# A macaron decoder layer on one core: FFN1's gain row and the gate weights loaded in an earlier group, and one late addition put behind the first block's rows

## The chip, the cores and the metric

The kernel runs on one core of a Trainium2 chip. The metric is the device time of one execution in microseconds (us). The core has a matrix engine, TensorE (PE; its weight loads are listed apart as PEld), a vector engine, VectorE (DVE), an engine for activation functions and scaled copies, ScalarE (ACT), a general engine, GpSimd (POOL), and a synchronising engine, SyncE (SP), which here only issues DMA transfers. POOL issues DMA transfers too, from its own queue. Every engine executes its instructions in program order and waits on semaphores for the others. 16 DMA engines move the data between HBM and the on-chip memory SBUF. Products of TensorE land in PSUM, eight banks of 128 x 512 float32.

## What is computed

One layer of a hybrid decoder: a half-step SwiGLU FFN, a mixer (a gated linear recurrence beside sliding-window attention), and a second half-step FFN, each between an RMSNorm on its input and one on its output. 512 tokens, width 1024, FFN width 2816, float32.

```python
def rms_norm(x, g):
    xf = x.astype(jnp.float32)
    y = xf * lax.rsqrt(jnp.mean(xf * xf, axis=-1, keepdims=True) + RMS_EPS)
    return (y * g.astype(jnp.float32)).astype(x.dtype)

def swiglu(x, w_gu, w_down):
    gate, up = jnp.split(x @ w_gu, 2, axis=-1)
    return (jax.nn.silu(gate) * up) @ w_down
...
    for l in range(DEPTH):
        x = x + 0.5 * rms_norm(swiglu(rms_norm(x, ffn1_pre_g[l]), ffn1_w_gu[l], ffn1_w_down[l]), ffn1_post_g[l])
        y = hybrid_mixer(rms_norm(x, mix_pre_g[l]), w_in[l], conv_w[l], conv_b[l], w_rg[l], b_rg[l],
                         w_ig[l], b_ig[l], lru_lambda[l], sinks[l], g_lru_out[l], g_attn_out[l], w_o[l])
        x = x + rms_norm(y, mix_post_g[l])
        x = x + 0.5 * rms_norm(swiglu(rms_norm(x, ffn2_pre_g[l]), ffn2_w_gu[l], ffn2_w_down[l]), ffn2_post_g[l])
```

In the mixer, `w_rg` and `w_ig` are block-diagonal gate weights, eight blocks of 64 x 64 each.

## The kernel before, in words

**Numbers.** Every float32 operand of a product is split into a high and a low part, and a product is three passes of TensorE: high times high, high times low, low times high. ScalarE makes the high parts (`act.copy`, the tiles `whi...`, `hha...`), VectorE the low parts (`wlo...`, `hla...`). The class `Weights` loads raw weights by SP into a ring of buffers and casts them a few units ahead of their use. A call of `take` hands the next unit to TensorE, and `W.later(n, fn)` registers a function that is issued after the n-th take from then on.

**FFN1.** Hidden columns are worked in groups of four chunks of 128 (`octo`, with seven products of half size in place of eight). The last group is `octo(16)`. Its result lies in `sqa` and is dealt into four blocks, `a11`, `a12`, `a21`, `a22` (tiles `ha`), by 16 small DMAs on SP and 16 on POOL (`place`, L992). The group before is multiplied with its down weights by `SevenDown.run`. Its partial sums are added to what earlier groups summed: some by a DMA that accumulates (L1105, POOL's queue, tiles `yp_a<-stage`), some by VectorE (L1097).

**The late addition.** In the last group `run` has `keep` set, and the banks of the last products stay in PSUM. For form `s1` the loop `for half in range(1 + i)` at L1095 adds bank 0 once and bank 1 twice, to the parts (1, 1) and (3, 1), counted by block of 128 tokens and half of the columns. The addition to part (3, 1) (`yp_a31`) also has to wait for an accumulating DMA to that part. It is the third of the three additions, and the part is not read before block 3.

**The end of FFN1, `boundary`.** The four blocks of 128 tokens are finished one by one. `produce(tb, dh)` issues the last down products of block `tb` and column half `dh`. `Rows.piece` adds the partial sum, squares it on ScalarE with a running sum (`sqyr`, L675), and multiplies by the gain row on VectorE (`zr`, L700). `Rows.steps` makes the residual sum (`x_rows`, L708) and the next norm (`sqxr`, `xn_r`). `Rows.turn` transposes the block on TensorE (`tp_r`, L729). TensorE runs ahead: the products of blocks 0 and 1 need only `a11` and `a12`; those of blocks 2 and 3 need `a21` and `a22`, and `whole.split` of these (L1397 on ScalarE, L1398 on VectorE) is issued in `produce(1, 0)`, behind all rows of block 0. `split_gates` (L1304 on ScalarE, L1305 on POOL) is issued in `produce(0, 1)`, ahead of block 0's second half. After the blocks, the first products of the mixer follow (`an`, L780, weights `whi_xl`, `wlo_xl`).

**Loads.** The constructor of `Rows` loads the gain row, spread over 128 partitions, into two tiles (L670, `grow_r`), and `load_gates` clears two tiles on POOL (L1295) and loads the gate weights into them by four DMAs on SP (L1298). Both are called after `octos` has issued the whole last group and its down products, so in SP's queue they stand behind the 16 DMAs of `ha`. All these tiles come from one ring of 41 buffers of 2 KB a partition (`t2k`): a load waits until the last reader of its buffer's former tile is done.

**FFN2** ends in the same way, in a loop of its own at the end of the program (L1923 on); its three additions to `yp_b` are at L1097 too, its gain row at L1920, its split of `a21` and `a22` after block 0's rows.

Of the kernel before, what the change touches and what calls it, by code (L numbers as in the profile page):

```python
# [15 lines left out]
P = 128  # L16
T = 512
NB = T // P
D = 1024
# [102 lines left out]
def tile_layer(ctx: ExitStack, tc: tile.TileContext, out: bass.AP, **ins: bass.AP):  # L122
# [465 lines left out]
    class Turned:  # L588
# [64 lines left out]
        def blocks(self):  # L653

            l, r = HALF
            for k in range(4):
# [2 lines left out]
                    pool.dma_start(b11[:, sl], x[:, l])  # L659
                self.t["b11", k] = b11[:, l], b11[:, r]  # L660

    class Rows:


        def __init__(self, name, x, gain, scale, eps, nxt, store=None):
            self.name, self.x, self.scale, self.eps, self.nxt, self.store = name, x, scale, eps, nxt, store
            self.z, self.ss, self.xn, self.tp = {}, {}, {}, {}
            self.grow = [t2k(f"grow_{name}{dh}") for dh in range(2)]
            for dh in range(2):
                sync.dma_start(self.grow[dh], ins[gain][0:1, dh * T:(dh + 1) * T].to_broadcast([P, T]))  # L670

        def sum_square(self, tb, dh, src, name):
            if dh == 0:
# [359 lines left out]
    class SevenDown:  # L1033
# [41 lines left out]
        def run(self, one, part, rest, keep=False):  # L1075
# [3 lines left out]
            for name, form, blocks in (("a", "a11", []), ("d", "s3", [(1, 1)]), ("b", "a12", [(0, 0)]), ("a", "s2", [(1, 0)]),  # L1079
# [10 lines left out]
                for i in range(2):  # L1090
                    if keep and form in ("a12", "s4", "a22"):
                        (half, dh), = blocks
                        kept[2 * half + i, dh] = banks[i]
                    elif keep and form == "s1":
                        for half in range(1 + i):  # L1095
                            o = part(half, 1, i)
                            dve.tensor_add(o, o, banks[i])  # L1097
                        if not i:
                            kept[2, 1] = banks[i]
                    else:  # L1100
                        st = wt("stage")
                        act.copy(st, banks[i])  # L1102
                        for half, dh in blocks:
                            o = part(half, dh, i)
                            pool.dma_start(o, st, accum_op=ALU.add)  # L1105
# [250 lines left out]
        for n, step in zip(takes, steps):  # L1356
            W.later(n, hid.place, step)

    def octos(hid, f0, f1, in_hbm, early=None):

        order = ("a11", "+s3", "s3", "a12", "+s1", "+s2", "s2", "+s4", "s4")
        parts = {}
        for f in range(f0, f1, 4):
            last = f == f1 - 4
            if last:
                for q in range(f1, FC, 2):
                    hid.quad(q, False, AHEAD)
                W.later(11, lambda: parts.update(read_parts(hid.name, in_hbm)))
            if f > f0:
                down = SevenDown(hid, f - 4)  # L1370
                down.ahead(zip((6, 6, 7, 8, 9, 9, 10, 11, 12) if f == f0 + 4 else (1, 2, 3, 4, 5, 6, 7, 8, 9), order))
# [92 lines left out]
    def produce(tb, dh):  # L1464
# [450 lines left out]
    for i in range(2):  # L1915
        load_rows(i, x_hbm, pool)
    preload(AF.Sqrt)
    grow = [t2k(f"grow{dh}") for dh in range(2)]
    for dh in range(2):
        sync.dma_start(grow[dh], ins["ffn2_post_g"][0:1, dh * T:(dh + 1) * T].to_broadcast([P, T]))  # L1920

    last = Last(f0, f1)
    for tb in range(NB):  # L1923
# [23 lines left out]
        if not tb:  # L1947
            for name in ("a21", "a22"):
                whole.split(name)
        if end:  # L1950
            dve.tensor_add(tot, tot, ss[:, 2:3])
        else:
            dve.tensor_add(tot, ss[:, 0:1], ss[:, 1:2])
# [36 lines left out]
```

## Time and profile before

| | us |
|---|---|
| median of three runs | 844.05 (843.65 to 845.2) |
| the profiled execution | 843.01 |
| its span, first to last instruction | 841.3 |
| TensorE busy | 821.8 (98%) |
| VectorE busy | 708.2 (84%) |
| ScalarE busy | 540.4 (64%) |
| GpSimd busy | 235.7 (28%) |
| mean granted clock of TensorE | 0.993 |

The times of rows in the profile are us from the span's start. A row of a timeline has start, duration, engine, source line, operation, `output<-inputs` by the program's names (without buffer numbers), the shape, and in brackets the engine's idle time before it with what ended that. The granted clock is the share of TensorE's full clock that the chip allowed it. A DMA share over 1 comes from transfers that overlap on one engine.

### The profile page before, as it was taken

The numbers are of one execution on the slowest core, as the hardware profiler recorded it, in microseconds if no ns is written. First come the engines' busy times: TensorE is split into PE (matmuls) and PEld (weight loads), VectorE is DVE, ScalarE is ACT, GpSimd is POOL, SyncE is SP. The second block draws the span as 40 slices with busy tenths as digits, with TensorE's granted clock in tenths as the row PEclk, the third lists the DMA queues.
The fourth block names the chain that finished last, engine by engine and source line by source line (L and its number), as shares of the span: only waits on it lengthen the run. The fifth ranks groups of instructions, "written<-read, shape, count | busy, mean of one in ns | idle before, by whom it ended". The sixth has DMA issues, their size and how long they took to land.

```text
span 841.3 us, 12066 instructions
## 1 busy us (share of the span) xinstructions
PE 821.8 (98%) x4156; PEld 693.4 (82%) x4156; DVE 708.2 (84%) x963; ACT 540.4 (64%) x905; POOL 235.7 (28%) x331
## 2 busy tenths in 40 slices
PE   9999999999999996999999999999999999999995
PEld 8888888888898885898788879888888888888884
DVE  4988889989979965767888767898998998899966
ACT  6756656665767563657857777674667677577542
POOL 2022004180460271005303103130418036055172
PEclk9999999999999998999999999999999999999998
DMA  8355316498694578032041344362549959589383
GB/s 251 102 194 206 132 69 203 115 206 253 145 240 118 198 183 231 10 92 95 6 101 51 125 175 176 136 209 106 157 148 209 263 136 202 188 195 245 140 210 113
DMA packets 90977, 133.22 MB, mean 158 GB/s; under 512 B 10600, under 2 KB 40612, under 8 KB 90916
## 3 DMA queue, kind: packets, MB, share of 16 engines
q1 hardware_dynamic: 69460, 91.41, 33.7%
q0 software_dynamic: 21312, 40.92, 22.6%
q8 instruction: 32, 0.52, 0.3%
q14 instruction: 29, 0.24, 0.1%
q10 hardware_dynamic: 144, 0.13, 0.0%
HBM read 93.10 MB, written 26.74 MB: 142 GB/s over the span
## 4 chain that ended last, share of the span: by engine, by line
PE 45%; ACT 6%; DVE 5%; DMA 1%; issue 1%; SPq 1%; POOL 0%; DVEq 0%; ACTq 0%
PE ab L935 12%; PE db L935 6%; PE bb L935 3%; PE an L780 1%; DMA x_rows<-x_hbm 1%; PE wo L1859 1%; PE mn L780 1%; PE yab L1336 1%; PE yab L1334 1%; PE yab L1335 1%; PE an L481 1%; PE gt L461 1%; PE sc L1571 1%; PE gt L463 1%; PE gt L462 1%
## 5 line engine op out<-in xcount | busy, mean ns | idle before, releaser
L1105 POOL DMA_DIRECT2D yp_b<-stage x46 | 44.6, 1308 | 93.4 <-ACT stage L1102 93.1
L992 POOL DMA_DIRECT2D hb<-sqb x80 | 48.4, 697 | 61.2 <-PE db L935 35.0
L992 POOL DMA_DIRECT2D ha<-sqa x64 | 39.0, 699 | 52.7 <-DVE sqa L950 44.4
L1105 POOL DMA_DIRECT2D yp_a<-stage x32 | 31.1, 1284 | 63.4 <-ACT stage L1102 60.6
L935 PE MATMUL aa<-whi_a_p,b_a 128*128 128x512 f32 x64 | 19.7, 389 | 0.0
L935 PE MATMUL ab<-whi_b_p,b_f 128*128 128x512 f32 x64 | 19.7, 389 | 0.0
L1522 POOL TENSOR_TENSOR xcl<-xc,xch 128x512 fp32r<-128x512 f32 x4 | 5.1, 1295 | 46.4 <-ACT xch L1521 46.4
L1610 POOL TENSOR_SCALAR_AFFINE_SELECT pc<-pa 128x384 f32<-128x384 f32 x8 | 5.6, 717 | 44.3 <-ACT pa L1609 43.6
L935 PE MATMUL db<-whi_b_q,t13h_f 128*128 128x512 f32 x40 | 15.6, 389 | 0.0
L935 PE MATMUL db<-whi_b_q,t13l_f 128*128 128x512 f32 x40 | 15.6, 389 | 0.0
L935 PE MATMUL db<-wlo_b_q,t13h_f 128*128 128x512 f32 x40 | 15.6, 389 | 0.0
L935 PE MATMUL ab<-whi_b_r,t24h_f 128*128 128x512 f32 x40 | 15.6, 389 | 0.0
L935 PE MATMUL ab<-whi_b_r,t24l_f 128*128 128x512 f32 x40 | 15.6, 389 | 0.0
L935 PE MATMUL ab<-wlo_b_r,t24h_f 128*128 128x512 f32 x40 | 15.6, 389 | 0.0
L935 PE MATMUL bb<-whi_b_s,xh_f 128*128 128x512 f32 x40 | 15.6, 389 | 0.0
L935 PE MATMUL bb<-whi_b_s,xl_f 128*128 128x512 f32 x40 | 15.6, 389 | 0.0
L935 PE MATMUL bb<-wlo_b_s,xh_f 128*128 128x512 f32 x40 | 15.6, 389 | 0.0
L935 PE MATMUL ab<-whi_b_t,t13h_f 128*128 128x512 f32 x40 | 15.6, 389 | 0.0
L935 PE MATMUL ab<-whi_b_t,t13l_f 128*128 128x512 f32 x40 | 15.6, 389 | 0.0
L935 PE MATMUL ab<-wlo_b_t,t13h_f 128*128 128x512 f32 x40 | 15.6, 389 | 0.0
L935 PE MATMUL db<-whi_b_u,t24h_f 128*128 128x512 f32 x40 | 15.6, 389 | 0.0
L935 PE MATMUL db<-whi_b_u,t24l_f 128*128 128x512 f32 x40 | 15.6, 389 | 0.0
(1536 smaller groups left out, 3266.0 us busy)
## 6 DMA issues: line engine op xcount, KB each, us to landing
yp_b<-stage POOLq DMA_DIRECT2D x54, 256.0 KB, 6.2
yp_a<-stage POOLq DMA_DIRECT2D x40, 256.0 KB, 6.6
raw_ad<-in_ffn_w_down SPq DMA_DIRECT2D x4, 1024.0 KB
hb<-sqb SPq DMA_DIRECT2D x80, 32.0 KB, 4.2
hb<-sqb POOLq DMA_DIRECT2D x80, 32.0 KB, 4.1
xn<-in_x SPq DMA_DIRECT2D x8, 256.0 KB, 3.0
ha<-sqa SPq DMA_DIRECT2D x64, 32.0 KB, 4.2
ha<-sqa POOLq DMA_DIRECT2D x64, 32.0 KB, 3.9
```

Of the source, the lines that this page charges most:

```text
L461: pe.matmul(ps, hi[:, k, :], xh, start=start, stop=False)
L462: pe.matmul(ps, hi[:, k, :], xl, start=False, stop=False)
L463: pe.matmul(ps, lo[:, k, :], xh, start=False, stop=stop)
L481: pe.matmul(sl(ps), w[:, k, :], xh, start=False, stop=False, skip_group_check=True)
L780: pe.matmul(l(b), w[part][:, k, :], l(xs[k][xpart]), start=k + part + xpart == 0, stop=stop and k == KD - 1)
L935: pe.matmul(o, x, w[:, k, :], start=first and i + k + j == 0, stop=i == 1 and k == 1 and j == 2, skip_group_check=True)
L992: (sync if i else pool).dma_start(o, squares[rows, 8 * pair + q:8 * pair + q + 5:4].rearrange("f c b t -> f c (b t)"))
L1105: pool.dma_start(o, st, accum_op=ALU.add)
L1334: pe.matmul(banks[i], hh[:, js], hi[:, k, :], start=first and k == 0, stop=False, skip_group_check=True)
L1335: pe.matmul(banks[i], hh[:, js], lo[:, k, :], start=False, stop=False, skip_group_check=True)
L1336: pe.matmul(banks[i], hl_[:, js], hi[:, k, :], start=False, stop=k == 1, skip_group_check=True)
L1571: pe.matmul(score_banks[j, n][i][:, o:o + keys.stop - keys.start], q_[pr, blk], k_[pr, keys], start=p == 0, stop=p == 2)
```

## The change

Three edits. First, loading the gain row is taken out of `Rows` into a function, `row_pieces`, which the three users call themselves. Second, for FFN1 that call and `load_gates` become a function `beside`, which `octos` registers for the 13th take of the last group. Third, the addition of bank 1 to part (3, 1) is no longer issued in `run`; it becomes `kept["late"]`, which FFN1 calls in `produce(1, 0)` behind the split of `a21` and `a22`, and FFN2 behind the same split after block 0's rows.

```diff
+    def row_pieces(gain):
+        grow = [t2k(f"grow_{gain}{dh}") for dh in range(2)]
+        for dh in range(2):
+            sync.dma_start(grow[dh], ins[gain][0:1, dh * T:(dh + 1) * T].to_broadcast([P, T]))
+        return grow
...
-        def __init__(self, name, x, gain, scale, eps, nxt, store=None):
+        def __init__(self, name, x, grow, scale, eps, nxt, store=None):
...
-            self.grow = [t2k(f"grow_{name}{dh}") for dh in range(2)]
-            for dh in range(2):
-                sync.dma_start(self.grow[dh], ins[gain][0:1, dh * T:(dh + 1) * T].to_broadcast([P, T]))
...
                     elif keep and form == "s1":
-                        for half in range(1 + i):
-                            o = part(half, 1, i)
-                            dve.tensor_add(o, o, banks[i])
-                        if not i:
+                        o = part(0, 1, i)
+                        dve.tensor_add(o, o, banks[i])
+                        if i:
+                            kept["late"] = lambda o=part(1, 1, i), b=banks[i]: dve.tensor_add(o, o, b)
+                        else:
                             kept[2, 1] = banks[i]
...
-    def octos(hid, f0, f1, in_hbm, early=None):
+    def octos(hid, f0, f1, in_hbm, early=None, beside=None):
...
                 W.later(11, lambda: parts.update(read_parts(hid.name, in_hbm)))
+                if beside:
+                    W.later(13, beside)
...
-    whole, parts, kept = octos(hid, *OCTO1, parts1)
+    grow1 = []
+
+    def beside():
+        grow1.extend(row_pieces("ffn1_post_g"))
+        load_gates()
+
+    whole, parts, kept = octos(hid, *OCTO1, parts1, None, beside)
...
-    rows1 = Rows("r1", x_rows, "ffn1_post_g", 4.0 / D, [eps4] * NB, mx)
-    load_gates()
+    rows1 = Rows("r1", x_rows, grow1, 4.0 / D, [eps4] * NB, mx)
...
         if (tb, dh) == (1, 0):
             for name in ("a21", "a22"):
                 whole.split(name)
+            kept["late"]()
...
-    rows2 = Rows("r2", x_rows, "mix_post_g", 1.0 / D, [post_eps[:, b:b + 1] for b in range(NB)], n2, store)
+    rows2 = Rows("r2", x_rows, row_pieces("mix_post_g"), 1.0 / D, [post_eps[:, b:b + 1] for b in range(NB)], n2, store)
...
-    grow = [t2k(f"grow{dh}") for dh in range(2)]
-    for dh in range(2):
-        sync.dma_start(grow[dh], ins["ffn2_post_g"][0:1, dh * T:(dh + 1) * T].to_broadcast([P, T]))
+    grow = row_pieces("ffn2_post_g")
...
         if not tb:
             for name in ("a21", "a22"):
                 whole.split(name)
+            kept["late"]()
```

How the instructions stand on SP at the end of FFN1, before. `raw_ad` and `raw_xl` are raw weights, `ha` the blocks of the last group, `grow_r` the gain row, `bd_w_rg` and `bd_w_ig` the gate weights:

```order
L168 DMA raw_ad_2817<-in_ffn_w_down 128x2x512
L992 DMA ha_2952<-sqa_2894 32x2x128 x4
L992 DMA ha_2961<-sqa_2894 32x2x128 x4
L992 DMA ha_2992<-sqa_2894 32x2x128 x4
L992 DMA ha_3001<-sqa_2894 32x2x128 x4
L168 DMA raw_ad_3076<-in_ffn_w_down 128x2x512
L168 DMA raw_xl__3114<-in_w_in 128x8x256
L670 DMA grow_r_3154<-in_ffn_post_g 128x512
L670 DMA grow_r_3155<-in_ffn_post_g 128x512
L1298 DMA bd_w_rg<-in_w_rg 64x4x64 x2
L1298 DMA bd_w_ig<-in_w_ig 64x4x64 x2
```

And with the change (the gain row's tiles are called `grow_ffn_post_g` now, and lines shift by a few):

```order
L168 DMA raw_ad_2817<-in_ffn_w_down 128x2x512
L665 DMA grow_ffn_post_g_2900<-in_ffn_post_g 128x512
L665 DMA grow_ffn_post_g_2901<-in_ffn_post_g 128x512
L1302 DMA bd_w_rg<-in_w_rg 64x4x64 x2
L1302 DMA bd_w_ig<-in_w_ig 64x4x64 x2
L995 DMA ha_2964<-sqa_2894 32x2x128 x4
L995 DMA ha_2973<-sqa_2894 32x2x128 x4
L995 DMA ha_3004<-sqa_2894 32x2x128 x4
L995 DMA ha_3013<-sqa_2894 32x2x128 x4
L168 DMA raw_ad_3088<-in_ffn_w_down 128x2x512
L168 DMA raw_xl__3126<-in_w_in 128x8x256
```

The six loads moved ahead of the 16 DMAs of `ha`. On POOL the two memsets of the gate tiles moved likewise, from behind the accumulating DMAs to a place directly behind the eight reads of the partial sums, ahead of `x_rows` and `ha`.

VectorE in FFN1, from the second of the three additions on to the first operation of block 1, with the rows of block 0 between left out, before:

```order
L1097 TENSOR_TENSOR yp_a_2849<-yp_a_2849,yaa_2936 128x512
L1097 TENSOR_TENSOR yp_a_2857<-yp_a_2857,yaa_2936 128x512
L193 TENSOR_TENSOR wlo_ad_3117<-raw_ad_2817,whi_ad_3116 128x1024
L191 SCALAR_TENSOR_TENSOR wlo_ad_3184<-raw_ad_3076,whi_ad_3183 128x1024
L693 TENSOR_TENSOR yp_a_2843<-yba_2937,yp_a_2843 128x512
...
L1398 TENSOR_TENSOR hla21a_3272<-ha_2992,hha21a_3271 128x512
L1398 TENSOR_TENSOR hla22a_3276<-ha_3001,hha22a_3275 128x512
L693 TENSOR_TENSOR yp_a_2847<-yba_2938,yp_a_2847 128x512
```

And with the change:

```order
L1099 TENSOR_TENSOR yp_a_2849<-yp_a_2849,yaa_2948 128x512
L193 TENSOR_TENSOR wlo_ad_3129<-raw_ad_2817,whi_ad_3128 128x1024
L191 SCALAR_TENSOR_TENSOR wlo_ad_3183<-raw_ad_3088,whi_ad_3182 128x1024
L696 TENSOR_TENSOR yp_a_2843<-yba_2949,yp_a_2843 128x512
...
L1404 TENSOR_TENSOR hla21a_3271<-ha_3004,hha21a_3270 128x512
L1404 TENSOR_TENSOR hla22a_3275<-ha_3013,hha22a_3274 128x512
L1101 TENSOR_TENSOR yp_a_2857<-yp_a_2857,yaa_2948 128x512
L696 TENSOR_TENSOR yp_a_2847<-yba_2950,yp_a_2847 128x512
```

The addition to `yp_a_2857` moved from ahead of the weights' low part to behind the split of `a22`.

VectorE at the end of FFN2, before:

```order
L1097 TENSOR_TENSOR yp_b_7773<-yp_b_7773,yab_7860 128x512
L1097 TENSOR_TENSOR yp_b_7781<-yp_b_7781,yab_7860 128x512
L1938 TENSOR_TENSOR yp_b_7767<-ybb_7861,yp_b_7767 128x512
L1936 SCALAR_TENSOR_TENSOR yp_b_7769<-yp_b_7769,yeb_7991 128x512
L1398 TENSOR_TENSOR hla21b_8095<-hb_7913,hha21b_8094 128x512
L1398 TENSOR_TENSOR hla22b_8099<-hb_7922,hha22b_8098 128x512
L1953 TENSOR_TENSOR tot_b_8061<-ss_b_8060 128x1
```

And with the change:

```order
L1099 TENSOR_TENSOR yp_b_7773<-yp_b_7773,yab_7860 128x512
L1948 TENSOR_TENSOR yp_b_7767<-ybb_7861,yp_b_7767 128x512
L1946 SCALAR_TENSOR_TENSOR yp_b_7769<-yp_b_7769,yeb_7991 128x512
L1404 TENSOR_TENSOR hla21b_8094<-hb_7913,hha21b_8093 128x512
L1404 TENSOR_TENSOR hla22b_8098<-hb_7922,hha22b_8097 128x512
L1101 TENSOR_TENSOR yp_b_7781<-yp_b_7781,yab_7860 128x512
L1964 TENSOR_TENSOR tot_b_8060<-ss_b_8059 128x1
```

Here the addition to `yp_b_7781` moved from ahead of block 0's first operation to behind both splits, directly ahead of the total of block 0's squares. TensorE and ScalarE issue the same instructions in the same order as before.

More of the change, by code (lines that the diff above doesn't have):

```diff
@@ L660, in blocks @@
                 self.t["b11", k] = b11[:, l], b11[:, r]
+    def row_pieces(gain):
[3 more added lines that the diff above has]
+        return grow
     class Rows:
-        def __init__(self, name, x, gain, scale, eps, nxt, store=None):
-            self.name, self.x, self.scale, self.eps, self.nxt, self.store = name, x, scale, eps, nxt, store
+        def __init__(self, name, x, grow, scale, eps, nxt, store=None):
+            self.name, self.x, self.grow, self.scale, self.eps, self.nxt, self.store = name, x, grow, scale, eps, nxt, store
             self.z, self.ss, self.xn, self.tp = {}, {}, {}, {}
-            self.grow = [t2k(f"grow_{name}{dh}") for dh in range(2)]
-            for dh in range(2):
-                sync.dma_start(self.grow[dh], ins[gain][0:1, dh * T:(dh + 1) * T].to_broadcast([P, T]))
         def sum_square(self, tb, dh, src, name):
```

## The prediction

> **What bounds the kernel now.** The page shows TensorE busy nearly throughout, but busy time counts whatever it does at whatever clock. I therefore read the waits of TensorE around the end of FFN1 first. The columns are: who waited for whom, total us, how often, longest.
>
> ```profile
> PE yda L1324 <- ACT hha21a L1397: 5.8, 1, 5.8
> ```
>
> This is the longest wait of TensorE in the whole program. TensorE stands still because ScalarE has not yet cast `a21` (tile `hha21a`) for block 2. The timeline of TensorE (start, duration, engine, line, tile, and in brackets the idle time before it and what ended it) gives the place, and a second, smaller gap:
>
> ```profile
> 311.68 0.39 PE L1326 MATMUL yba<-whi_ad,hla12a 128*128 128x512 f32 x1
> ...
> 315.30 0.39 PE L1324 MATMUL yba<-whi_ad,hha 128*128 128x512 f32 x1
> 316.68 0.50 PE L1325 MATMUL yba<-wlo_ad,hha 128*128 128x512 f32 x1 [0.99 <-DVE wlo_ad L193]
> ...
> 317.95 0.40 PE L1324 MATMUL yea<-whi_ad,hha 128*128 128x512 f32 x1
> ...
> 327.25 0.39 PE L1326 MATMUL yea<-whi_ad,hla 128*128 128x512 f32 x1
> 333.43 0.80 PE L1324 MATMUL yda<-whi_ad,hha21a 128*128 128x512 f32 x1 [5.79 <-ACT hha21a L1397]
> ...
> 338.42 0.40 PE L1324 MATMUL yda<-whi_ad,hha 128*128 128x512 f32 x1
> ```
>
> From 317.95 to 327.25 there are 41 steps, so an undisturbed matmul takes 0.227 us. From 333.43 to 338.42 there are 12 steps at 0.416 us. The stretch after the gap has this row (busy us of PE, PEld, DVE, ACT, POOL with counts, then granted clock, DMA share, GB/s):
>
> ```profile
> 333.40:338.40 5.00, 4.97 (x12) 3.90 (x13) 4.07 (x9) 2.24 (x6) 1.16 (x2) 0.53 0.01 3
> ```
>
> The granted clock is 0.53 there: after the long gap TensorE restarts at half speed, which costs 4.99 - 12 x 0.227 = 2.27 us on top of the gap. After the 0.99 us gap it does not.
>
> Why is ScalarE late? VectorE first, then ScalarE, whose queue holds the cast behind block 0's whole post-norm:
>
> ```profile
> 308.99 0.69 DVE L1398 TENSOR_TENSOR hla12a<-ha,hha12a 128x512 fp32r<-128x512 f32 x1 [0.94 <-ACT hha12a L1397]
> 309.60 1.28 DVE L1097 TENSOR_TENSOR yp_a<-yp_a,yaa 128x512 f32<-128x512 f32 x2
> 314.81 0.69 DVE L1097 TENSOR_TENSOR yp_a<-yp_a,yaa 128x512 f32<-128x512 f32 x1 [3.92 <-DMA yp_a<-stage]
> 315.41 1.22 DVE L193 TENSOR_TENSOR wlo_ad<-raw_ad,whi_ad 128x1024 fp32r<-128x1024 f32 x1
> ...
> 318.14 0.69 DVE L693 TENSOR_TENSOR yp_a<-yba,yp_a 128x512 f32<-128x512 f32 x1 [0.38 <-PE yba L1326]
> 323.85 0.69 DVE L700 TENSOR_TENSOR zr<-yp_a,grow_r 128x512 f32<-128x512 f32 x1 [5.01 <-DMA grow_r<-in_ffn_post_g]
> ...
> 334.02 0.68 DVE L1398 TENSOR_TENSOR hla22a<-ha,hha22a 128x512 fp32r<-128x512 f32 x1
> 334.62 0.68 DVE L693 TENSOR_TENSOR yp_a<-yba,yp_a 128x512 f32<-128x512 f32 x1
> ```
>
> ```profile
> 313.44 1.06 ACT L183 ACTIVATE whi_ad<-raw_ad 128x1024 fp32r<-128x1024 f32 x1 [2.97 <-DMA raw_ad<-in_ffn_w_down]
> 318.87 0.63 ACT L675 ACTIVATE sqyr<-yp_a 128x512 f32<-128x512 f32 x1 [4.37 <-DVE yp_a L693]
> ...
> 325.65 0.62 ACT L1304 CAST hi_w_rg<-bd_w_rg 128x512 fp32r<-128x512 f32 x1 [6.05 <-DMA bd_w_rg<-in_w_rg]
> ...
> 332.78 0.60 ACT L1397 CAST hha21a<-ha 128x512 fp32r<-128x512 f32 x1
> ```
>
> Three waits are visible. The late addition (314.81) waits 3.92 us for an accumulating DMA, and `wlo_ad`, which TensorE needs at 315.53, stands behind it. The gain row reaches VectorE only at 323.85. The gate weights reach ScalarE at 325.65, and everything up to `hha21a` follows in its queue: 332.78 - 325.65 = 7.13 us of work. Gates and gain row are parallel delays of one chain; they do not add up.
>
> **The change, part by part.**
>
> *Loads moved forward.* SP and POOL now issue them ahead of the blocks `ha` of the last group. The SP queue before, and then the last of the four earlier users of the buffers that they now take (read from the waits of the built program):
>
> ```profile
> 296.83 10.93 SPq L992 DMA_DIRECT2D ha<-sqa  x16
> ...
> 309.31 2.86 SPq L670 DMA_DIRECT2D grow_r<-in_ffn_post_g  x2
> ...
> 317.19 2.44 SPq L1298 DMA_DIRECT2D bd_w_ig<-in_w_ig  x2
> ```
>
> ```profile
> 282.21 0.39 PE L935 MATMUL da<-whi_a_u,t24l_a 128*128 128x512 f32 x1
> ```
>
> The buffers are free at 282.6. Before, the six DMAs kept SP from 309.31 to 319.63, that is 10.3 us, in a crowded stretch; at that slow pace they are issued by 293, and `ha` starts at 296.83. What the DMA engines do meanwhile (same columns as above):
>
> ```profile
> 280.00:285.00 5.00, 5.00 (x24) 4.14 (x23) 4.59 (x6) 2.59 (x3) 1.23 (x3) 1.00 1.03 389
> 285.00:290.00 5.00, 5.00 (x24) 4.14 (x23) 4.42 (x6) 2.44 (x3) 0.00 (x0) 1.00 0.29 109
> 290.00:295.00 5.00, 5.00 (x24) 4.14 (x23) 5.00 (x7) 2.57 (x5) 0.37 (x1) 1.00 0.00 0
> ```
>
> Two tiles of 256 KB and four pieces of 64 KB are 0.79 MB, 2.0 us at 389 GB/s; the engines stand almost empty from 285 to 295. I cost the move at nothing, with that emptiness as its cover; without it the price is that of the last rival. POOL's two memsets move too, past `x_rows` and `ha`, and are over long before 294.
>
> *The chain of block 0 in FFN1.* Step by step, old time to new:
> - `wlo_ad` follows the two remaining additions at 310.81 instead of 315.41 and is done at 312.0. TensorE no longer waits at 315.53. The first `yea` matmul comes at 315.30 + 6 x 0.227 = 316.66 instead of 317.95: 1.29 us earlier.
> - The next one that could be late is the second half of that weight. ScalarE's cast waits for its DMA and ends at 314.50; with 1.2 us for its rest it is there at 315.7, ahead of 316.9. No wait.
> - `yp_a` on VectorE follows TensorE: 318.14 becomes 316.85. ScalarE's `sqyr` becomes 317.58 and is over some 0.7 us later. With the gates loaded, `hi_w_rg` follows there: 318.34 instead of 325.65, 7.31 us earlier. The gain row is loaded too, so nothing of block 0 waits behind it.
> - `hha21a` ends at 333.38 - 7.31 = 326.07. TensorE reaches it at 327.25 + 0.23 - 1.29 = 326.19. The gap closes but for some 0.2 us (the rest of `a21` comes 0.7 us after its cast).
> - So TensorE starts `yda` 333.43 - 326.19 = 7.24 us earlier, and without a long gap it keeps its clock: 2.27 us more. Taken alone, TensorE would be 9.3 us ahead after 338.42 (with 0.2 lost to the `a21` gap).
>
> *What is late next.* The late addition stands behind `hla22a` now: 0.60 us of VectorE (334.02 to 334.62 is the step of such an operation). So block 1 starts 7.31 - 0.60 = 6.7 us earlier, and this chain is now behind TensorE. It meets TensorE once more at its other idle times, first VectorE and then ScalarE and TensorE:
>
> ```profile
> 341.68 0.68 DVE L693 TENSOR_TENSOR yp_a<-yda,yp_a 128x512 f32<-128x512 f32 x1
> ...
> 343.01 0.42 DVE L1314 CAST up<-upf 128x512 uint8<-128x512 f32 x1
> 344.99 0.69 DVE L691 SCALAR_TENSOR_TENSOR yp_a<-yp_a,yaa 128x512 f32<-128x512 f32 x1 [1.57 <-PE yaa L1326]
> ```
>
> ```profile
> 359.10 1.98 ACT L185 CAST whi_xl<-raw_xl__3175 128x1024 fp32r<-128x1024 f32 x2
> ```
>
> ```profile
> 360.39 2.15 PE L780 MATMUL an<-xh_mx,whi_xl 128*128 128x256 f32 x16
> ```
>
> VectorE waited 1.57 us for `yaa` in block 2. TensorE's `yaa` is 9.3 us earlier, so this wait goes: `up` ends at 343.43 - 6.7 = 336.7, and `yp_a` starts there instead of at 344.99, 8.3 us earlier. From there VectorE and ScalarE run in one chain to the cast `whi_xl` at 359.10. Its first half, one of two in 1.98 us, ends at about 360.1, and TensorE used it at 360.39, a slack of 0.2 to 0.3. TensorE would come 9.3 us earlier, the cast only 8.3: TensorE waits some 0.7 us, and **FFN1's gain is 8.3 + 0.2 = 8.5 us**. A gap of 0.7 us leaves the clock alone, as the one of 0.99 did. After it TensorE leads, and what follows moves as one.
>
> *FFN2.* The same addition moves behind `hla22b`. VectorE first, TensorE's last matmul second:
>
> ```profile
> 812.78 0.69 DVE L1097 TENSOR_TENSOR yp_b<-yp_b,yab 128x512 f32<-128x512 f32 x1 [1.58 <-DMA yp_b<-stage]
> ...
> 815.95 0.69 DVE L1936 SCALAR_TENSOR_TENSOR yp_b<-yp_b,yeb 128x512 f32<-128x512 f32 x1 [1.88 <-PE yeb L1326]
> ...
> 817.94 1.38 DVE L1398 TENSOR_TENSOR hla21b<-hb,hha21b 128x512 fp32r<-128x512 f32 x1 [1.30 <-ACT hha21b L1397]
> 819.24 0.68 DVE L1398 TENSOR_TENSOR hla22b<-hb,hha22b 128x512 fp32r<-128x512 f32 x1
> 819.84 0.15 DVE L1953 TENSOR_TENSOR tot_b<-ss_b 128x1 f32<-128x1 f32 x1
> ```
>
> ```profile
> 832.10 0.28 PE L1326 MATMUL ybl<-whi_bd,hla22b 128*128 128x256 f32 x1
> ```
>
> Before, the addition stood in a stretch where VectorE waited for TensorE anyway (1.88 us idle at 815.95), so taking it out gains nothing. Behind `hla22b` it stands on the path that ends the program: after 819.84 VectorE and ScalarE follow each other to the last store, and TensorE is done at 832.38, early. I take its step, 0.60 us, as a **loss of 0.6 us**. The bounds are 0 (some later idle time swallows it) and 1.4 (it is drawn out as `hla21b` was, 1.38 us for the same shape).
>
> *The sum.* 8.5 - 0.6 = 7.9 us. The profiled execution took 843.01 us (span 841.3), so 835.1. The median of the three runs, 844.05, lies 1.04 above it; I carry the difference over: **836.1 us**.
>
> The clock is the term that the trace shows only once. [...]
>
> **The rivals.**
>
> *The chain of block 0 stays late.* Something else arrives late, for instance the second `raw_ad` (ScalarE waited 2.97 us for it at 313.44) or casts that now meet POOL's work. A delay d of the chain takes d from the gain, since the chain is the bound up to 360. With d = 3 that is 839.1. If a gap of more than some us remains before `yda`, half clock comes back: with a gap of 3.4 us, the middle between 0.99 us (no drop) and 5.79 us (drop), TensorE starts at 329.6, 3.8 us early, keeps the slow stretch, and gives 844.05 - 3.8 + 0.6 = 840.8. For it: a margin of 0.1 us at `hha21a`. Against: every step keeps its order, and DMA traffic in that stretch becomes less. Chance 0.13. [...]
>
> *The change does not do what it says.* The loads would land early, but the wait moves to another input of the same step, and the time stays, with FFN2's 0.6 us on top: 844.6. Nothing in block 0's chain shows such an input. Chance 0.04.
>
> *Slower.* The place is SP's queue: 16 DMAs of `ha` stand behind the six loads, and the loads wait for buffers and memsets. If they were issued only from 296.83 on, `ha` would be 10.3 us late. The slack is that of `hla12a`: done at 309.68, used at 311.68, 2.0 us. TensorE would stand 8.3 us there, lose 2.3 to the clock, gain 8.5 later and pay 0.6: +2.7, 846.8 us. Up to 2.0 us of delay cost nothing, and from about 7.6 on the change is a loss. The rows at 282.21 and 290 speak against it: 3.8 us of margin at the slowest pace seen. Chance 0.04.
>
> [...]
>
> **How the numbers follow.** The forecast of 836.1 has 0.79, the three rivals 0.13, 0.04 and 0.04. The low end is TensorE's own 9.3 us with FFN2's step hidden: 844.05 - 9.3 = 834.75, so 834.6. The high end takes in a chain that is late by 3 us: 839.2. A measurement of this kernel can tell some 0.2%, or 1.7 us, from no change. All of the forecast and of the first rival lie beyond it on the fast side: faster 0.92, same 0.04, slower 0.04.
>
> **What would show it.** Right: no wait of `zr` for `grow` and of `hi_w_rg` for its DMA; `hi_w_rg` near 318.3; `yda` near 326.3 behind a gap well under 1 us, at clock 1.00; a wait near 0.7 us of TensorE for `whi_xl`; in FFN2 the addition directly behind `hla22b` and everything after it 0.6 us later against that instruction. Wrong: `ha` issued later than 297; a new wait for `raw_ad`; a stretch of half clock that remains; a FFN2 end that does not move by the 0.6 us.

## The result, and the profile after

The changed kernel takes 836.25 us (median of six executions, 834.85 to 841.01) against 844.18 us before (843.65 to 845.2, six executions). The ratio is 0.991, with a 95% interval of 0.989 to 0.9935: **faster by 7.9 us**. The profiled execution took 837.13 us, with a span of 835.4 us.

The waits of TensorE around the end of FFN1, in the changed kernel:

```profile
PE yea L1329 <- DVE wlo_ad L191: 0.8, 1, 0.8
PE an L783 <- ACT whi_xl L185: 0.4, 1, 0.4
```

The 5.8 us for `hha21a` and the 0.99 us in `yba` are gone; two short waits took their place. The same in TensorE's timeline, and behind it the stretch after `yda`, with the two stretches into which the loads moved (columns as in the prediction):

```profile
311.82 0.39 PE L1330 MATMUL yba<-whi_ad,hla12a 128*128 128x512 f32 x1
...
318.36 0.50 PE L1329 MATMUL yea<-wlo_ad,hha 128*128 128x512 f32 x1 [0.76 <-DVE wlo_ad L191]
...
327.56 0.39 PE L1330 MATMUL yea<-whi_ad,hla 128*128 128x512 f32 x1
327.79 0.39 PE L1328 MATMUL yda<-whi_ad,hha21a 128*128 128x512 f32 x1
...
353.10 2.17 PE L783 MATMUL an<-xh_mx,whi_xl 128*128 128x256 f32 x16 [0.37 <-ACT whi_xl L185]
```

```profile
285.00:290.00 5.00, 5.00 (x24) 4.14 (x23) 4.33 (x7) 2.30 (x3) 0.00 (x0) 1.00 0.97 293
290.00:295.00 5.00, 5.00 (x23) 4.14 (x23) 5.00 (x7) 2.58 (x5) 0.22 (x1) 1.00 0.03 5
327.80:332.80 5.00, 5.00 (x28) 4.17 (x27) 4.12 (x9) 1.81 (x6) 1.17 (x2) 1.00 0.11 34
```

`yda` follows the step before it after 0.23 us, at a granted clock of 1.00 (0.53 before). The moved loads fill the formerly almost empty 285 to 290 (share 0.97, before 0.29) and are all but over at 290 (0.03 behind it). SP's queue, then ScalarE and VectorE:

```profile
280.28 2.15 SPq L665 DMA_DIRECT2D grow_ffn_post_g<-in_ffn_post_g  x2
282.91 1.39 SPq L1302 DMA_DIRECT2D bd_w_rg<-in_w_rg  x2
284.39 1.33 SPq L1302 DMA_DIRECT2D bd_w_ig<-in_w_ig  x2
296.97 11.14 SPq L995 DMA_DIRECT2D ha<-sqa  x16
308.52 0.62 SPq L168 DMA_DIRECT2D raw_ad<-in_ffn_w_down  x1
```

```profile
310.94 1.22 DVE L193 TENSOR_TENSOR wlo_ad<-raw_ad,whi_ad 128x1024 fp32r<-128x1024 f32 x1
...
315.99 1.06 ACT L183 ACTIVATE whi_ad<-raw_ad 128x1024 fp32r<-128x1024 f32 x1 [5.37 <-DMA raw_ad<-in_ffn_w_down]
...
318.95 0.69 DVE L703 TENSOR_TENSOR zr<-yp_a,grow_ffn_post_g 128x512 f32<-128x512 f32 x1
...
319.58 0.61 ACT L1308 CAST hi_w_rg<-bd_w_rg 128x512 fp32r<-128x512 f32 x1
...
326.74 0.60 ACT L1403 CAST hha21a<-ha 128x512 fp32r<-128x512 f32 x1
...
328.58 0.68 DVE L1101 TENSOR_TENSOR yp_a<-yp_a,yaa 128x512 f32<-128x512 f32 x1
```

`zr` and `hi_w_rg` wait for no load any more, and `ha` is issued where it was. But the cast of the second `raw_ad`, at 313.44 before, starts at 315.99, and `hi_w_rg` behind it comes 1.2 us later than predicted. The end of FFN2, VectorE and GpSimd:

```profile
808.53 0.69 DVE L1946 SCALAR_TENSOR_TENSOR yp_b<-yp_b,yeb 128x512 f32<-128x512 f32 x1 [2.03 <-PE yeb L1330]
...
811.73 0.68 DVE L1101 TENSOR_TENSOR yp_b<-yp_b,yab 128x512 f32<-128x512 f32 x1
812.10 1.29 POOL L1956 TENSOR_TENSOR yp_b<-yp_b,grow_ffn_post_g 128x512 f32<-128x512 f32 x1 [7.35 <-DMA grow_ffn_post_g<-in_ffn_post_g]
812.33 1.08 DVE L1964 TENSOR_TENSOR tot_b<-ss_b 128x1 f32<-128x1 f32 x1
814.04 2.54 DVE L1971 SCALAR_TENSOR_TENSOR yp_b<-yp_b,rs_b,x_rows 128x512 f32<-128x512 f32 x2
816.50 0.68 DVE L1948 TENSOR_TENSOR yp_b<-ybb,yp_b 128x512 f32<-128x512 f32 x1
```

The late addition takes its 0.60 us here, and then the total (128x1) takes 1.08 us instead of 0.15, and the residual sum 2.54 us instead of 1.42, beside GpSimd's product, which came late because FFN2's gain row landed late. Before, the same residual sum and the operation behind it:

```profile
820.62 1.42 DVE L1960 SCALAR_TENSOR_TENSOR yp_b<-yp_b,rs_b,x_rows 128x512 f32<-128x512 f32 x2
821.95 0.69 DVE L1938 TENSOR_TENSOR yp_b<-ybb,yp_b 128x512 f32<-128x512 f32 x1
```

**A common measure.** The start of a span wanders from profile to profile (the first `yba<-whi_ad,hla12a` lies between 310.98 and 312.19), so each run is read between matmuls. FFN1's gain is how much shorter the way from the first `yba<-whi_ad,hla12a` (311.68 before, 311.82 after) to the `an` of the chain (360.39 and 353.10) became: 48.71 - 41.28 = 7.43 us. FFN2's end is read from VectorE's operation on `yeb` to its next one on `ybb`: 815.95 to 821.95 before, 6.00 us, and 808.53 to 816.50 after, 7.97 us.

### The profile page after: what moved, and what is told of

It is laid out like the page before. It is cut to its first block, busy times and chain, and to the rows that moved or that the text cites. A ratio compares the mean times of both kernels' runs of the same rounds, so it can differ in the third digit from the quotient of the medians.

```text
span 835.4 us, 12062 instructions
## 1 busy us (share of the span) xinstructions
PE 819.9 (98%) x4156; PEld 692.2 (83%) x4156; DVE 710.1 (85%) x963; ACT 541.0 (65%) x905; POOL 235.6 (28%) x331
## 4 chain that ended last, share of the span: by engine, by line
PE 38%; DVE 9%; ACT 9%; issue 2%; DMA 1%; POOL 1%; DVEq 0%; ACTq 0%; POOLq 0%
PE ab L938 12%; PE db L938 7%; PE bb L938 3%; PE yab L1338 1%; PE yab L1339 1%; DMA x_rows<-x_hbm 1%; PE yab L1340 1%; PE wo L1871 1%; PE mn L783 1%; PE an L481 1%; ACT sc L1604 1%; PE ydb L1338 1%; PE ydb L1340 1%; PE ydb L1339 1%; PE an L783 1%
## 5 line engine op out<-in xcount | busy, mean ns | idle before, releaser
L1949 ACT ACTIVATE ysq<-yp_b 128x512 f32<-128x512 f32 (+1 forms) x9 | 5.2, 582 | 16.9 <-DVE yp_b L1948 14.3
```

Of the source, the lines that this page charges most:

```text
L1949: act.activation(wt(f"ysq{tb}{i}")[:, :c1 - c0], y, AF.Square, accum_out=ss[:, i:i + 1])
```

## The experiments

The **theory**: the loads carry the gain, as two parallel delays of one chain; the late addition gives nothing as long as the second `raw_ad` lands late, and costs its step twice. The **rivals**: the addition's move has a gain of its own; one of the two loads was the whole delay. Edits are against the changed kernel. The ratio is to the kernel before, timed again beside each group of runs: e1 to e4, e5 to e8, e9 to e11, and e12. The last three columns are from one profile each.

| run | median us (n) | ratio, 95% | cast of `raw_ad` | FFN1's gain | FFN2's end |
|---|---|---|---|---|---|
| changed | 836.25 (6) | 0.991, 0.989 to 0.9935 | 315.99 | 7.4 | 7.97 |
| e1 loads only | 834.09 (6) | 0.988, 0.986 to 0.990 | 314.93 | 8.6 | 6.58 |
| e2 addition only | 844.30 (12) | 1.0004, 0.999 to 1.002 | 315.83 | -1.3 | 6.37 |
| e3 gates only | 839.12 (8) | 0.994, 0.992 to 0.996 | 316.64 | 2.5 | 5.80 |
| e4 gain row only | 842.34 (12) | 0.998, 0.997 to 0.999 | 317.10 | 2.1 | 6.15 |

**e1**: the addition back in its old place, in both FFNs.

```diff
-                        o = part(0, 1, i)
-                        dve.tensor_add(o, o, banks[i])
-                        if i:
-                            kept["late"] = lambda o=part(1, 1, i), b=banks[i]: dve.tensor_add(o, o, b)
-                        else:
+                        for half in range(1 + i):
+                            o = part(half, 1, i)
+                            dve.tensor_add(o, o, banks[i])
+                        if not i:
...
-            kept["late"]()
```

> Only the loads are moved; the late addition is back in its old place in both FFNs. Theory (the loads carry the gain; in the profile of the changed kernel block 0's chain was already bound by the second raw_ad, so the addition's old place costs nothing more): the 0.99 us gap of TensorE before its first use of the weight behind the addition comes back, hi_w_rg still comes near 319.6, yda stays without a gap of over 1 us, FFN1's gain stays 7 to 7.5 us, and FFN2's loss of 0.6 to 2 us goes. Time 834.5 to 836, ratio to before 0.989 to 0.990. Rival (the addition's move is worth its 1.29 us of TensorE, the prediction's first step): 837 to 838, ratio 0.992 or more.

Measured: 834.09 us, the theory's time. The whole gain is there without the addition's move, and rather more. Its waits of TensorE are down to one, and none for `whi_xl`:

```profile
PE yea L1328 <- DVE wlo_ad L191: 0.6, 1, 0.6
```

FFN1's gain is 8.6 us, so one detail of the expectation (7 to 7.5) was too low: block 1's chain saves the addition's 0.6 us, and `raw_ad` landed 1.1 us earlier.

Another detail was missed: the gap of 0.99 us in `yba` does not come back, although the addition is in its old place. The accumulating transfer for which it waits landed earlier than in the profile of before, where the addition started at 314.81:

```profile
312.85 0.69 DVE L1100 TENSOR_TENSOR yp_a<-yp_a,yaa 128x512 f32<-128x512 f32 x1 [2.29 <-DMA yp_a<-stage]
```

The low part behind it is done at 314.68, ahead of TensorE's first use at 315.21. In e3, e4 and e8 the addition is in its old place too; it starts at 312.86, 312.42 and 313.83, and TensorE does not wait in `yba` either. So in none of these four profiles was there a gap for the addition's move to close. Whether the moved loads brought that transfer forward, or it was late by chance in the one profile of before, is not shown.

The end of FFN2 is 6.58 us and not the 6.00 of before: here VectorE waits 1.18 us for GpSimd's second product, which waited 3.68 us for the gain row.

**e2**: only the addition moved. The order of loads is that of before.

```diff
-    whole, parts, kept = octos(hid, *OCTO1, parts1, None, beside)
+    whole, parts, kept = octos(hid, *OCTO1, parts1)
...
+    beside()
     rows1 = Rows("r1", x_rows, grow1, 4.0 / D, [eps4] * NB, mx)
```

> Only the late addition is moved, in both FFNs; gain row and gate weights are loaded where they were. Theory (gain row and gate weights bound block 0's chain): the 0.99 us gap goes but the wait of TensorE for hha21a grows from 5.8 to about 7 us, so FFN1 ends as before, and FFN2 loses 0.6 to 2 us: 844.8 to 846.2, ratio 1.001 to 1.0025. Rival (the addition's move has a gain of its own): 843 or less, ratio under 0.999.

Measured: no gain, 844.30 us, 0.5 us under the lower end of the theory and far from the rival. Its waits:

```profile
ACT hi_w_rg L1308 <- DMA bd_w_rg<-in_w_rg: 6.9, 1, 6.9
PE yda L1328 <- ACT hha21a L1403: 6.7, 1, 6.7
DVE zr L703 <- DMA grow_ffn_post_g<-in_ffn_post_g: 5.8, 1, 5.8
```

What TensorE saves early it stands longer before `yda`, and since both loads and `raw_ad` landed later than in the profile of before, FFN1 is 1.3 us longer in this one. And the cast of `raw_ad` starts at 315.83 here, with the loads where they always were: its landing is late without the change.

**e3 and e4**: the loads moved one at a time, with the addition in its old place.

```diff
     def beside():
-        grow1.extend(row_pieces("ffn1_post_g"))
         load_gates()
...
+    grow1.extend(row_pieces("ffn1_post_g"))
     rows1 = Rows("r1", x_rows, grow1, 4.0 / D, [eps4] * NB, mx)
```

(e3; in e4 the gain row stays in `beside`, and `load_gates()` goes behind `Rows`.)

> Only the gate weights are moved; gain row and late addition are where they were. Theory (two parallel delays of one chain): zr still waits for the gain row until about 323.9, the second sqyr comes near 325.1 instead of 326.7, so the gain is about 1.6 us (up to 3 if the gain row lands earlier without the gate weights behind it): 841.2 to 842.8, ratio 0.9965 to 0.998. TensorE's wait before yda stays over 2.5 us. Rival (the gates alone were the delay): a gain of 6 us or more, 838 or less.

> Only the gain row is moved; gate weights and late addition are where they were. Theory (two parallel delays): zr waits no more, hi_w_rg still waits for its load until 322.2 (issued 3.4 us earlier and landing so much earlier) to 325.7 (landing unmoved), and the gain is that shift, 0 to 3.4 us: 840.7 to 844.2, ratio 0.996 to 1.000. With the run that moves only the gate weights the two gains together stay under the 7.3 us of both. Rival (the gain row alone was the delay): 838 or less.

Measured: 839.12 us and 842.34 us. In FFN1 the gates alone bring 2.5 us and the gain row alone 2.1; together 4.6, where both bring 8.6. So they are two delays side by side, and only the removal of both frees the chain. The clock alone does not explain it: from the first `yba<-whi_ad,hla12a` to the start of `yda`, a way in which no matmul ran at half clock, e3 is 1.95 us shorter than before, e4 1.66 and e1 6.36. The rest of the gains, 0.6, 0.4 and 2.3 us, comes behind that, where e3 and e4 still have a stretch of half clock and e1 has none. e4 is within its expectation; e3 is 2 us faster than expected; its profile shows 0.9 of that in FFN1, where the residual sum `x_rows` took 1.42 us instead of 2.22, and the rest is a few tenths each at the start, between the FFNs and at the end. The surprise of e3 is the clock. TensorE's wait before `yda`, and then the windows:

```profile
331.07 0.67 PE L1327 MATMUL yda<-whi_ad,hha21a 128*128 128x512 f32 x1 [2.49 <-ACT hha21a L1402]
```

```profile
330.00:331.00 1.00, 0.00 (x0) 0.00 (x0) 0.28 (x1) 1.00 (x3) 0.00 (x0) 1.00 0.00 0
331.00:332.00 1.00, 0.93 (x3) 0.58 (x4) 0.95 (x2) 0.54 (x2) 0.00 (x0) 0.62 0.00 0
332.00:333.00 1.00, 1.00 (x4) 0.81 (x4) 0.96 (x3) 0.00 (x0) 0.00 (x0) 0.50 0.00 0
333.00:334.00 1.00, 1.00 (x4) 0.81 (x3) 1.00 (x2) 0.72 (x2) 0.12 (x1) 0.50 0.08 16
334.00:335.00 1.00, 1.00 (x4) 0.77 (x4) 0.27 (x1) 0.63 (x2) 0.94 (x2) 0.67 0.00 0
335.00:336.00 1.00, 1.00 (x6) 0.78 (x6) 0.84 (x4) 0.39 (x2) 0.10 (x1) 1.00 0.00 0
```

Here a wait of 2.49 us brought half clock, for (0.38 + 0.5 + 0.5 + 0.33) x 2 = 3.4 us. The wait of 2.65 us in e4 did the same. The prediction had set the point in the middle, at 3.4.

**e5 to e8**: where the addition costs, and whether `raw_ad` can be had earlier.

| run | median us (n) | ratio, 95% | cast of `raw_ad` | FFN1's gain | FFN2's end |
|---|---|---|---|---|---|
| e5 changed, again | 836.06 (6) | 0.992, 0.989 to 0.994 | 314.69 | 7.9 | 6.66 |
| e6 FFN2's addition back | 836.88 (6) | 0.992, 0.989 to 0.994 | 315.43 | 7.7 | 6.58 |
| e7 `raw_ad` ahead of `x_rows` | 835.97 (5) | 0.990, 0.989 to 0.992 | 316.18 | 7.6 | 6.39 |
| e8 = e1, FFN2's row early | 835.43 (6) | 0.991, 0.9885 to 0.993 | 315.88 | 8.4 | 6.00 |

> The changed kernel once more, beside the next three runs. Both theories: 835.5 to 837, ratio 0.990 to 0.9925. If the second raw_ad lands where it likes from run to run, its cast whi_ad starts somewhere from 313.4 to 317.1 us again (it was 313.4 in the kernel before, and 315.0 to 317.1 in five profiles since, two of them without the moved loads); if the moved loads delay it, it starts at 315.5 or later.

Measured: the same time again, and the cast at 314.69. It lies between 314.7 and 317.1 in nine profiles (changed and e1 to e8), one of them without moved loads; the 313.44 of before was the earliest of ten. It is late without the moved loads too (315.83 in e2), and with them it came before 315.5 here, so nothing shows that they delay it. The order of loads of before has only two profiles, though, 313.44 and 315.83.

e6:

```diff
-                        if i:
+                        if i and n[0] == "b":
+                            o = part(1, 1, i)
+                            dve.tensor_add(o, o, banks[i])
+                        elif i:
                             kept["late"] = lambda o=part(1, 1, i), b=banks[i]: dve.tensor_add(o, o, b)
```

(FFN2's `kept["late"]()` goes too.)

> The changed kernel with the late addition of FFN2 alone back in its old place; FFN1 as changed. Theory (the addition costs FFN2 its step of 0.6 us and up to 1.4 us more where it pushes the total against GpSimd's products): 1 to 2 us faster than the changed kernel, 834.3 to 835.3, ratio 0.988 to 0.990, and FFN1's rest, 0.6 us for block 1, still there against the run that moves the loads alone. Rival (FFN2's place is neutral, the difference to the run with the loads alone is FFN1's): the same as the changed kernel within 0.4 us.

Measured: nearest the rival. The time does not fall (three of the six executions took 838.4 to 839.2), and FFN2's end is 6.58 us against 6.66 in e5. With the addition in its old place VectorE waits for GpSimd's product instead, which waits for the gain row:

```profile
812.10 1.67 POOL L1959 TENSOR_TENSOR yp_b<-yp_b,grow_ffn_post_g 128x512 f32<-128x512 f32 x1 [3.76 <-DMA grow_ffn_post_g<-in_ffn_post_g]
813.81 0.75 DVE L1973 SCALAR_TENSOR_TENSOR yp_b<-yp_b,rs_b,x_rows 128x512 f32<-128x512 f32 x1 [1.18 <-POOL yp_b L1959]
```

e7 takes the second half of `x_rows` from ahead of `raw_ad`:

```diff
-    W.later(77, lambda: W.owed.extend(lambda i=i: load_rows(i, ins["x"][0], pool) for i in range(2)))
+    def rows_of(i):
+        return lambda: load_rows(i, ins["x"][0], pool)
+
+    W.later(77, lambda: W.owed.extend((rows_of(0), W.load, rows_of(1))))
```

> The changed kernel, with the second raw_ad taken ahead of the second half of x_rows in the order of loads, so that 1 MB less is in flight ahead of it. Theory (raw_ad lands late because it shares the DMA engines with x_rows and the accumulating transfers, and TensorE's wait of 0.8 us for its low part hangs on it): whi_ad starts at 314.0 or earlier, TensorE's wait in yea is under 0.2 us, hi_w_rg comes at 318.6 or earlier, and the time is 0.7 to 1.3 us below the changed kernel of the same call. Rival (its landing is set elsewhere): the cast still starts at 315 or later and the time stays.

Measured: the theory falls. `raw_ad` is still issued at 308.71, behind all of `ha`, its cast starts at 316.18, and the time stays. GpSimd issues the second half of `x_rows` at 310.29 now and not at 307.95, so that half is not what delays `raw_ad`. The accumulating transfers stayed ahead of it and are not tested here.

e8:

```diff
-    whole, parts, kept = octos(hid, *OCTO2, parts2, first_part)
+    grow = []
+    whole, parts, kept = octos(hid, *OCTO2, parts2, first_part, lambda: grow.extend(row_pieces("ffn2_post_g")))
...
-    grow = row_pieces("ffn2_post_g")
```

> The run with the loads alone (late addition in its old place in both FFNs), and FFN2's gain row loaded at the 13th take of FFN2's last group as FFN1's is. Theory (at the end the second product of GpSimd with the gain row waits for its load, 3.7 us in the profile of the loads alone, and VectorE waits 1.2 us for that product): GpSimd's wait for the row goes, VectorE's wait for GpSimd too, 1 to 1.5 us less than the loads alone: 832.6 to 833.2, ratio 0.9865 to 0.9875. Rival (something else, such as x_rows from HBM, is as late): within 0.4 us of the loads alone, ratio 0.988 or more.

Measured: the waits go as expected, and FFN2's end is 6.00 us, 0.6 under e1. The time does not show it: 835.43 us where 832.6 to 833.2 was expected, with two of the six executions at 837.9 and 840.1. The step is shown in the profile alone.

**e9 to e11**: `raw_ad` really early. In e9, on top of e7's edit:

```diff
-                placed(hid, (1, 1, 2, 2), (0, 2, 1, 3))
+                placed(hid, (1, 1, 6, 6) if hid.name == "a" else (1, 1, 2, 2), (0, 2, 1, 3))
```

e10 is e1 with this, e7's and e8's edits; e11 is the same, with FFN1's addition moved as in the change.

| run | median us (n) | ratio, 95% | cast of `raw_ad` | FFN1's gain | FFN2's end |
|---|---|---|---|---|---|
| e9 changed, `raw_ad` early | 834.95 (4) | 0.989, 0.988 to 0.991 | 309.68 | 8.7 | 6.87 |
| e10 addition in place, all early | 833.92 (4) | 0.988, 0.986 to 0.9895 | 309.82 | 7.8 | 6.00 |
| e11 FFN1's addition moved, all early | 834.55 (4) | 0.989, 0.9875 to 0.990 | 310.64 | 8.7 | 5.99 |

> The changed kernel, with the second raw_ad taken ahead of the second half of x_rows and the 16 + 16 DMAs of ha for a21 and a22 moved behind it (they are registered for the 6th take instead of the 2nd; SP issued them for over 4 us ahead of raw_ad). Theory (TensorE's wait of 0.7 to 0.8 us in yea, and with it about a microsecond of FFN1's gain, hang on when raw_ad is issued): raw_ad is issued at 305.5 or earlier instead of 308.5, whi_ad starts at 311 or earlier, the wait in yea is gone, yda comes 0.6 to 1.2 us earlier against the start of the span than in the changed kernel, and the time is 0.5 to 1.2 us lower, 834.8 to 835.6. Rival (the accumulating transfers, which come earlier too, hold the DMA engines until the same time): whi_ad still at 314 or later, the time as the changed kernel or, if a21 and a22 are late now, slower.

Measured: the theory. SP issues `raw_ad` at 301.90, and the cast, in ScalarE's timeline, waits no more:

```profile
309.68 1.05 ACT L183 ACTIVATE whi_ad<-raw_ad 128x1024 fp32r<-128x1024 f32 x1
```

TensorE waits neither in `yba` nor in `yea`, FFN1's gain is 8.7 us, and the median is 1.1 to 1.3 us below those of the changed kernel (the intervals overlap). What had delayed it is its place in SP's queue, behind the `ha` of blocks that are needed much later: issued 6.6 us earlier, it lets its cast start 6.3 us earlier. The edit moves more than this transfer: GpSimd, too, issues the accumulating transfers ahead of half of its `ha`, at 301.40 and not at 306.73 and 310.11.

> The loads moved, the late addition in its old place in both FFNs, FFN2's gain row early as in e8, and raw_ad ahead as in e9. Theory (three waits are gone: raw_ad in FFN1, the gain row in FFN2, and the late addition's 0.6 us steps): 832.8 to 834.2, ratio 0.986 to 0.9885; what is left in FFN1 is the wait of TensorE behind the late addition, 0 to 1 us. Rival (what is removed was hidden by another wait): 834.1 or more, as with the loads alone.

> As e10, but FFN1's late addition moved as in the change (FFN2's in its old place). With raw_ad early the addition's place decides when TensorE has its weights, as the prediction's first step has it. Theory of that step: no wait of TensorE in yba or yea, yda up to 1 us earlier than in e10, but block 1's chain 0.6 us later, and a wait of some 0.7 us for whi_xl: about the same time as e10 within 0.6 us. Rival (the addition's move is a gain once raw_ad is early): over 0.8 us below e10.

Measured: 833.92 and 834.55 us, 0.63 us apart, with intervals that overlap, so the addition's place is worth nothing measurable here. But the addition has nothing to wait for in e10, as the accumulating transfers come earlier there; its three additions follow each other:

```profile
309.04 1.88 DVE L1100 TENSOR_TENSOR yp_a<-yp_a,yaa 128x512 f32<-128x512 f32 x3
```

The pair therefore does not price the move where that transfer is late. e10 is the fastest version, some 10 us below before and 2.1 to 2.3 us below the changed kernel; its interval (up to 0.9895) and those of the changed kernel (from 0.989) still touch, and it is level with e1. FFN1's gain is only 7.8 us in e10, for one operation. VectorE's and GpSimd's timelines:

```profile
319.40 1.29 POOL L1308 TENSOR_TENSOR lo_w_rg<-bd_w_rg,hi_w_rg 128x512 fp32r<-128x512 f32 x1
319.44 2.50 DVE L684 TENSOR_TENSOR toty_r<-ssy_r 128x1 f32<-128x1 f32 x1 [1.09 <-ACT sqyr L678]
320.64 1.28 POOL L1308 TENSOR_TENSOR lo_w_ig<-bd_w_ig,hi_w_ig 128x512 fp32r<-128x512 f32 x1
```

An addition of 128x1 lasts 2.50 us, until GpSimd's two operations end, and TensorE waits 1.1 us before `yda` behind it.

**e12**: `raw_ad` later still.

```diff
-    W.later(77, lambda: W.owed.extend(lambda i=i: load_rows(i, ins["x"][0], pool) for i in range(2)))
+    W.later(77, lambda: W.owed.extend(lambda i=i: load_rows(i, ins["x"][0], sync if i else pool) for i in range(2)))
```

> The changed kernel, with the second half of x_rows (1 MB) loaded by SP directly ahead of the second raw_ad, so that raw_ad lands later. In e1 to e8 its cast started between 314.7 and 317.1 us, and single executions of the changed kernel took 839 to 841 us at a mean clock of 0.990 to 0.995, where the others took 835 to 837. Theory (those executions are ones in which raw_ad lands some 3 us later, and a wait of TensorE of 2.5 us or more in yea brings half clock with it): the cast starts at 318 to 320, TensorE waits 2.5 to 4.5 us in yea, the granted clock falls to 0.5 for some 3.4 us behind it, and the median is 838.5 to 842. Rival 1 (the delay is a plain loss): the same cast, no stretch of half clock, 837.5 to 839. Rival 2 (the landing is bound by the accumulating transfers and not by what SP has ahead): the cast stays at 314.7 to 317.1 and the time at 835.5 to 837.

Measured: the theory, 841.39 us (839.75 to 842.62, eleven executions; ratio 0.997, 0.996 to 0.998), but the half clock lasts 6.8 us, where 3.4 us were expected. TensorE's wait, and its clock in the windows behind it:

```profile
320.46 0.80 PE L1328 MATMUL yea<-whi_ad,hha 128*128 128x512 f32 x1 [4.19 <-ACT whi_ad L183]
```

```profile
316.00:320.00 4.00, 0.27 (x2) 0.00 (x0) 0.00 (x0) 0.65 (x1) 0.00 (x0) 0.97 1.08 332
320.00:324.00 4.00, 3.07 (x6) 2.12 (x7) 2.52 (x3) 2.11 (x5) 0.38 (x1) 0.50 1.10 348
324.00:326.00 2.00, 2.00 (x6) 1.59 (x5) 0.95 (x2) 0.78 (x3) 2.00 (x2) 0.50 1.10 349
326.00:328.00 2.00, 2.00 (x9) 1.54 (x9) 1.97 (x5) 0.60 (x2) 0.60 (x2) 0.85 0.43 136
```

With the cast 3.4 us later (319.35), 5 us of the gain are lost. That makes a late `raw_ad` a possible cause of the single executions of 837.9 to 841 us, eight of 35 in the changed kernel and its relatives with a late `raw_ad` (e1, e5 to e8), none of twelve in e9 to e11. The mean granted clock speaks for it in three of the eight (0.990 to 0.992, where most of e12 has 0.991), and not in the other five (0.993 to 0.996, where the 27 faster ones have 0.994 to 0.997). None of the eight was profiled, so this stays open.

## Why the prediction was right, and where not

The time was right: 836.1 us predicted, 836.25 measured. The reason was right in its main part, the loads; that the two numbers agree so closely is in part luck. Point by point:

- **The loads fit the empty stretch.** Right: SP is done with them at 285.7, `ha` starts at 296.97 (296.83 before), and the share of 0.97 ends by 290. The rival from SP's queue did not occur.
- **Gates and gain row are parallel delays of one chain.** Right, and shown by e3, e4 and e1: 2.5, 2.1 and 8.6 us.
- **`wlo_ad` follows the two additions, no wait at 315.53.** Right: 310.94, and no gap in `yba`. But it is worth nothing by itself (e2), and e1 has the whole gain without it: the gap of 0.99 us rested on the landing of one accumulating transfer in one execution, and in e1, e3, e4, e8 and e10 it is absent with the addition in its old place. What the move is worth when that transfer is late and nothing else is, no run shows.
- **"The next one that could be late is the second half of that weight ... No wait."** This step failed. It took the landing of `raw_ad` from one execution, 313.44, as given; nine other profiles have 314.7 to 317.1. In the changed kernel the cast started at 315.99, TensorE waited 0.76 us in `yea`, `hi_w_rg` came at 319.58 instead of 318.3, and `yda` at 327.79 instead of 326.3. The first rival named this very transfer; it came with d = 1.2 at `hi_w_rg` instead of 3. e9 takes it away, and FFN1's gain is 8.7 us, where the sum had 8.5.
- **The clock term.** Right: `yda` follows without a wait, at 1.00. The bound that the rival set for a drop, 3.4 us, was too high: 2.49 us sufficed in e3.
- **What is late next.** Right in kind: the addition costs block 1's chain its 0.60 us (328.58 to 329.18), and TensorE waits for `whi_xl`, 0.37 us instead of 0.7. With the addition in its old place there is no such wait (e1).
- **FFN2's loss of 0.6 us.** Mis-sized in the profiled execution: its end grew by 1.97 us, over the upper bound of 1.4, because the gain row landed late and GpSimd's products (from 812.10 and from 814.08) then ran beside VectorE's total and residual sum: 0.60 for the addition, 0.93 for the total and 1.12 for the residual sum, less 0.69 as `hla21b` took 0.69 us and not 1.38. In e5, e7 and e9, with the same order, it grew by 0.66, 0.39 and 0.87. The cover that e6 shows was not thought of: with a late row the addition's old place is no better (6.58).
- **The sum.** For the profiled execution it was 835.1, and 837.13 was measured: FFN1 gave 1.1 less and FFN2 took 1.4 more than stated, and some tenths elsewhere went the other way. The terms were thus 2.0 us too low. The prediction then added 1.04 us, because the median of before lay that much above its profiled execution; after, the median lies 0.9 below it. These two errors cancel, and that is luck: the agreement of 836.1 with 836.25 is closer than the terms are.

## What to carry to other kernels

Where several loads end a wait of one chain, move all of them or expect little: here the single ones brought 2.5 and 2.1 us, and both together 8.6. A transfer's landing in one profile is not to be taken as a constant (the cast of `raw_ad` started at 313.44 in one profile and from 314.7 to 317.1 in nine); a step that rests on a margin of 1 us against it needs the landing of several profiles, or the transfer issued ahead of what is needed later. Before an operation is moved off one engine's path, look for what else arrives at the same time: here the next weight and the next row were as late as the work that was moved away.

## What the runs showed of the hardware

**The clock fell after shorter waits than assumed.** TensorE's waits of 0.76 us (the changed kernel), 0.99 us (before), 1.12 us (e10) and 1.3 us (e3) left the granted clock at 1.00. Between 1.3 and 2.49 us, only e4 has a wait from 300 to 365 us (1.4 us), without a reading of the clock around it. 2.49 us (e3) brought 0.50 for 3.4 us, and so did 2.65 us (e4: 0.79, 0.50, 0.50 and 0.51 in the four windows of 1 us from 331.7 on). 4.19 us (e12) brought it for (0.03 x 4 + 2 + 1 + 0.15 x 2) x 2 = 6.8 us, as long as the 5.79 us of before (0.61 in the window from 331 to 332, 0.50 to 338, 0.97 to 339) and the 6.7 us of e2 (0.90 from 331.5 to 332.5, 0.50 to 338.5, 0.69 to 339.5). So the half clock lasted 3.4 us in two of these five stretches and 6.8 us in three; what sets its length, no run shows.

**A tiny operation of VectorE lasted as long as GpSimd's work beside it.** A total of 128x1 took 0.15 us with no GpSimd operation beside it (819.84, before). In the changed kernel's FFN2 end it took 1.08 us, to 813.41, where GpSimd's product ended at 813.39. In e10 it took 2.50 us, to 319.44 + 2.50 = 321.94, where the second of two GpSimd operations ended at 320.64 + 1.28 = 321.92; that second one began 1.20 us after the total. Each of these GpSimd operations has two inputs. What holds such a total back, no run shows.
